# A streamed fp32 matmul with scale and add on one core: 28 transfers in place of 39, and the last pairs of tiles off TensorE

## The chip, the core and the metric

The kernel runs on one core of a Trainium2 chip. A core has TensorE (PE in the profile, with its weight loads shown apart as PEld), VectorE (DVE), ScalarE (ACT), GpSimd (POOL) and SyncE (SP); here SP does nothing but issue the transfers between the chip's main memory and the on-chip memory, and 16 DMA engines carry them. The metric is the device time of the launch in microseconds, lower is better. Each kernel is timed in several runs and the median is taken; one more execution is recorded by the hardware profiler.

## The reference

```python
batch, m, k, n = 16, 512, 1024, 768
x          = randn(batch, m, k)   # float32
weight     = randn(k, n)          # float32
scale      = 0.1
add_value  = randn(batch, m, n)   # float32

return (scale * np.matmul(x, weight) + add_value).astype(np.float32)
```

With the batch flattened, `x` is 8192 x 1024 and the output 8192 x 768. A tile is 128 rows, so there are T = 64 tiles. In float32, a tile of `x` has 0.524 MB, a tile of `add_value` or of the output 0.393 MB, and `weight` has 3.15 MB. All data crosses the memory once: 33.55 MB of `x`, 25.17 MB of `add_value`, 3.15 MB of `weight`, 25.17 MB of output, 87.03 MB in all.

## The kernel before

**Layout.** `rows` views the rows in groups of 8 tiles (G = 8): inside a group a partition holds 8 neighbouring rows of memory, one for each tile. So a transfer of n tiles of one group reads, for each of the 128 partitions, one run of n rows: 4,096 bytes times n for `x`, 3,072 bytes times n for `add_value` and the output.

**Buffers.** `xs` has 16 slots for tiles of `x` in fp32 (tile t lies in slot t % 16). `ao` has 32 slots of 768 columns, which hold `add_value`, are overwritten in place by the result, and are stored from there (tile t in slot t % 32). At the start the last 8 slots of `ao` take the fp32 weight, and the three before them (21 to 23, `EARLY_AT`) the scaled products of the first three tiles. `w_bf` is the weight in bf16.

**Work on a tile.** The product needs `x` with k on the partitions, in bf16. There are two ways to it.

- *Through TensorE*: POOL (for the first three tiles DVE with ACT or POOL) casts the tile to bf16 (`cast_to`, L130; `xb_pool` has 3 buffers), TensorE transposes it in 4 pieces, taking two bf16 values as one fp32 (`transpose`, L156), and DVE or ACT copies the result from PSUM to `xt` (L164). ACT does the copy for tiles 0 to 3 and, before, for the tiles after the last moved pair.
- *Off TensorE* (a moved pair, `move_pair` and `turn_moved`): ACT or POOL casts two tiles in 16 instructions of 32 partitions x 512 elements, four in each of four steps, which also moves 32-row blocks between partitions (L118), and DVE turns 32 x 32 blocks in one instruction (L126). `MOVED_ACT` and `MOVED_POOL` list the first tiles of these pairs; each of the two engines has two buffers (`va_pool`, `vp_pool`).

A tile's product is 16 matmuls (8 steps of k, 512 and 256 columns each), into one of 3 PSUM buffers (`mm_pool`). `finish` (L185) is one DVE instruction: product times scale plus `ao`, written to `ao`.

**Order.** The order is written out by hand. `STREAM` lists all transfers: `x` and `w` load, `a` loads `add_value`, `o` stores the output (`l` and `r`: its left and right columns). SP issues them in this order, and a transfer whose slots are not free yet holds up those behind it. The loop at L248 walks through the list and, ahead of each entry, emits as many steps of the computation as the entry needs: a load of `x` over slots in use needs all their casts and moves, a store needs `finish` of its tiles. A load of `add_value` over slots in use waits for the store from them to land.

`head` does the first three tiles (EARLY = 3) while the weight comes in, one k step at a time, with `add_value` added afterwards (`added`, L245). From tile 3 on, `step` does one tile t: half of its matmuls, the transposes of tile t + 1 if that isn't in a moved pair, the casts up to tile t + 4, a quarter of the move of the pairs that start at t + 8, t + 7, t + 6 and t + 5, the other half of the matmuls, `finish`, and last, if a moved pair starts at t + 4, its turn on DVE. So on DVE the turn of pair t + 4 stands between `finish` of t and `finish` of t + 1. The last tile's matmuls and `finish` are split by columns.

Of the kernel before, what the change touches and what calls it, by code (L numbers as in the profile page):

```python
# [9 lines left out]


STREAM = [
    ("x", 0, 3), ("w", 0, 2), ("w", 2, 2), ("w", 4, 2), ("x", 3, 1), ("w", 6, 2),
    ("a", 0, 3), ("x", 4, 4), ("a", 3, 1), ("a", 4, 4), ("x", 8, 4), ("x", 12, 4),
    ("x", 16, 4), ("a", 8, 8), ("x", 20, 4), ("x", 24, 8), ("o", 0, 8), ("a", 16, 8),
    ("x", 32, 8), ("a", 24, 8), ("a", 32, 8), ("x", 40, 8), ("o", 8, 8), ("x", 48, 8),
    ("a", 40, 8), ("o", 16, 8), ("x", 56, 8), ("a", 48, 8), ("o", 24, 8), ("o", 32, 8),
    ("a", 56, 8), ("o", 40, 8), ("o", 48, 8), ("o", 56, 4), ("o", 60, 1), ("o", 61, 1),
    ("o", 62, 1), ("l", 63, 1), ("r", 63, 1),
]  # L20

X_SLOTS = 16
# [3 lines left out]
EARLY = 3  # L26

MOVED_ACT = [14, 18, 22, 26, 30, 34, 38, 42, 46, 50, 54, 58]  # L30
MOVED_POOL = [16, 20, 24, 28, 32, 36, 40, 44, 48, 52, 56]


@with_exitstack
def kernel(
# [8 lines left out]
    nc = tc.nc  # L44
    P = 128
# [19 lines left out]
    def rows(view, s, n):  # L65
        assert s // G == (s + n - 1) // G
        return view[:, s // G, s % G:s % G + n, :]


    w_v = weight.rearrange("(c p r) n -> p c r n", p=P, r=2)  # L70

    const = ctx.enter_context(tc.tile_pool(name="const", bufs=1))
    xb_pool = ctx.enter_context(tc.tile_pool(name="xb_pool", bufs=XB_BUFS))
# [12 lines left out]
    ao = const.tile([P, A_SLOTS, N], fp32, name="ao")  # L86
    w_bf = const.tile([P, KJ, N], bf16, name="w_bf")

    xb_tiles, xt_tiles, mm_tiles, done = {}, {}, {}, {"cast": 0, "step": 0, "x": 0}
    in_pair = {t0 + i: t0 for t0 in MOVED_ACT + MOVED_POOL for i in range(2)}  # L90
    moved, cast_pairs = {}, set()

    def load_w(j, n):

        s = A_SLOTS - KJ + j
        if n == 1:
            nc.sync.dma_start(ao[:, s, :], w_v[:, j // 2, j % 2, :])
        else:
            nc.sync.dma_start(ao[:, s:s + 2, :], w_v[:, j // 2, :, :])  # L99
        for i in range(n):  # L100
            nc.vector.tensor_copy(w_bf[:, j + i, :], ao[:, s + i, :])  # L101

    def move_pair(t0, a):


        act = t0 in MOVED_ACT
        if a == 0:
# [22 lines left out]
    def cast_to(t):  # L130
        while done["cast"] <= t:
            i = done["cast"]
            if i in in_pair:
                assert in_pair[i] in cast_pairs
                done["cast"] += 1
                continue
            if len(xb_tiles) == XB_BUFS:
                break
            xb = xb_pool.tile([P, K], bf16, tag="xb")
            src = xs[:, i % X_SLOTS, :]  # L140
            if i < EARLY:
                nc.vector.tensor_copy(xb[:, 0:K // 2], src[:, 0:K // 2])  # L142
                other = nc.gpsimd.tensor_copy if i else nc.scalar.copy
                other(xb[:, K // 2:K], src[:, K // 2:K])  # L144
            else:
                nc.gpsimd.tensor_copy(xb, src)  # L146
            xb_tiles[i] = xb
            done["cast"] += 1

    def transpose(t, pieces=1):  # L150
        cast_to(t)

        pairs = xb_tiles.pop(t).bitcast(fp32)
        tp = tp_pool.tile([P, KC, P], fp32, tag="tp")
        for c in range(KC):
            nc.tensor.transpose(tp[:, c, :], pairs[:, c * P:(c + 1) * P], identity)  # L156
        if t % 2 == 0:
            xt = xt_pool.tile([P, 2, KC, P], fp32, tag="xt")
            for i in range(2):
                xt_tiles[t + i] = xt[:, i, :, :]  # L160
        q = KC // pieces
        evacuate = nc.scalar.copy if t <= EARLY or t > LAST_PAIR else nc.vector.tensor_copy
        for c in range(0, KC, q):
            evacuate(  # L164
                xt_tiles[t][:, c:c + q, :].bitcast(bf16), tp[:, c:c + q, :].bitcast(bf16))
# [25 lines left out]
    def head(op, s, n):  # L191


        for i in range(s, s + n):
            if op == "x" and i < EARLY:
                transpose(i, 2)
                have_x.append(i)
                for j in have_w:
                    product(i, j, BOTH)
            elif op == "w":  # L200
                if i == KJ - 1:
                    transpose(EARLY)
                have_w.append(i)
                for t in have_x:
                    product(t, i, BOTH)
        if len(have_w) == KJ and len(have_x) == EARLY and not done["step"]:
            for t in range(EARLY):

                if t == 1:
                    nc.scalar.mul(  # L210
                        ao[:, EARLY_AT + t, :], mm_tiles[t, BOTH[0]][:, 0:N], float(scale))
                else:
                    nc.vector.tensor_scalar(  # L213
                        ao[:, EARLY_AT + t, :], mm_tiles[t, BOTH[0]][:, 0:N], float(scale), None,
                        op0=mybir.AluOpType.mult)
            done["step"] = EARLY

    LAST_PAIR = max(in_pair)
    EARLY_AT = A_SLOTS - KJ - EARLY

    def step():
        t = done["step"]
        if t < T - 1:
            for j in range(KJ):
                if j == KJ // 2:
                    if t + 1 not in in_pair:
                        transpose(t + 1)
                    cast_to(min(t + AHEAD, done["x"] - 1))
                    for a in range(4):
                        if in_pair.get(t + 8 - a) == t + 8 - a:  # L230
                            move_pair(t + 8 - a, a)
                product(t, j, BOTH)
            finish(t, BOTH[0], 0, N)
            if in_pair.get(t + 4) == t + 4:
                turn_moved(t + 4)
        else:
            for cols in BOTH:
                for j in range(KJ):
                    product(t, j, [cols])
                finish(t, cols, *cols)  # L240
        done["step"] += 1

    def added(t):
        assert done["step"] >= EARLY
        nc.vector.tensor_add(  # L245
            ao[:, t, :], ao[:, EARLY_AT + t, :], ao[:, t, :])

    for op, s, n in STREAM:  # L248
        last = s + n - 1
        if op == "w":  # L250
            load_w(s, n)
            head(op, s, n)
        elif op == "x":
            if last >= X_SLOTS:
                while done["cast"] <= last - X_SLOTS:
                    step()
            k = s % X_SLOTS
            nc.sync.dma_start(xs[:, k:k + n, :], rows(x_v, s, n))  # L258
            done["x"] = s + n
            if last < EARLY:  # L260
                head(op, s, n)
        elif op == "a":
            k = s % A_SLOTS
            nc.sync.dma_start(ao[:, k:k + n, :], rows(add_v, s, n))  # L264
            for t in range(s, min(s + n, EARLY)):
                added(t)
        else:
            while done["step"] <= last:
                step()
            k = s % A_SLOTS  # L270
            n0, n1 = {"o": (0, N), "l": (0, CUT), "r": (CUT, N)}[op]
            nc.sync.dma_start(rows(out_v, s, n)[:, :, n0:n1], ao[:, k:k + n, n0:n1])  # L272
# [35 lines left out]
```

## Time and profile before

| | |
|---|---|
| median of 3 runs | 210.14 us (209.95 to 210.92) |
| the profiled execution | 210.28 us |
| its span, first to last instruction | 208.5 us |
| TensorE busy, granted clock (mean) | 181.6 us, 0.96 |
| DVE, ACT, POOL busy | 101.3, 129.0, 124.3 us |
| DMA: bytes, mean rate over the span | 87.21 MB, 418 GB/s |
| transfers in `STREAM` | 39 |

The span is what the profile covers; the device time of the same execution is 1.8 us longer. Busy time is the time in which an engine executes instructions; for the 16 DMA engines it is the mean over them. The profile's page has, beside these, a picture of the span in 40 slices of 5.2 us, the share of each DMA queue, the chain of waits that ended last, and the groups of instructions by line; the trace also holds each transfer's issue, each packet's size and duration, and the moment at which each of the 16 engines finished its part of a transfer.

### The profile page before, as it was taken

The numbers are of one execution on the slowest core, as the hardware profiler recorded it, in microseconds if no ns is written. First come the engines' busy times: TensorE is split into PE (matmuls) and PEld (weight loads), VectorE is DVE, ScalarE is ACT, GpSimd is POOL, SyncE is SP. The second block draws the span as 40 slices with busy tenths as digits, with TensorE's granted clock in tenths as the row PEclk, the third lists the DMA queues.
The fourth block names the chain that finished last, engine by engine and source line by source line (L and its number), as shares of the span: only waits on it lengthen the run. The fifth ranks groups of instructions, "written<-read, shape, count | busy, mean of one in ns | idle before, by whom it ended". The sixth has DMA issues, their size and how long they took to land.

```text
span 208.5 us, 2886 instructions
## 1 busy us (share of the span) xinstructions
PE 181.6 (87%) x1096; PEld 110.7 (53%) x1096; DVE 101.3 (49%) x111; ACT 129.0 (62%) x206; POOL 124.3 (60%) x199
## 2 busy tenths in 40 slices
PE   0599399980899997999999999999999999989960
PEld 0455256650466664566666666666666666656630
DVE  0536535511466514855655555555553685233330
ACT  2423000499959798599999999999999900003210
POOL 1310524379898980999998899999999960001000
PEclk9999889996589999999999999999999999999997
DMA  6999999999999999999999999999999999999995
GB/s 236 415 428 440 413 429 434 421 450 406 454 418 448 407 429 462 404 443 420 442 434 413 461 418 424 420 429 437 421 434 424 432 439 424 429 418 439 429 394 214
DMA packets 5629, 87.21 MB, mean 418 GB/s; under 512 B 624, under 2 KB 752, under 8 KB 2032
## 3 DMA queue, kind: packets, MB, share of 16 engines
q1 hardware_dynamic: 5616, 87.03, 98.2%
q8 instruction: 8, 0.13, 0.3%
q14 instruction: 5, 0.04, 0.0%
HBM read 61.87 MB, written 25.17 MB: 417 GB/s over the span
## 4 chain that ended last, share of the span: by engine, by line
DMA 75%; ACT 9%; PE 7%; DVE 3%; SPq 1%; issue 1%; DVEq 0%
DMA out_dram<-ao 35%; DMA ao<-in_add_value_dram 22%; DMA xs<-in_x_dram 13%; ACT va L118 9%; PE mm L177 6%; DMA ao<-in_weight_dram 5%; DVE ao L185 2%; DVE xt L126 1%; PE tp L156 1%; SPq L258 1%; SPq L99 0%; SPq L264 0%; SPq L272 0%; DVEq L185 0%
## 5 line engine op out<-in xcount | busy, mean ns | idle before, releaser
L177 PE MATMUL mm<-w_bf,xt 128*128 128x256 bf16 (+1 forms) x1024 | 173.8, 331 | 8.8 <-DVE xt L164 6.6
L177 PEld LDWEIGHTS <-xt 128*128 128x128 bf16 x1024 | 101.3, 99 | 76.9 <-DVE xt L164 7.0
L118 ACT CAST va<-xs 32x512 bf16<-32x512 f32 x192 | 118.2, 616 | 28.8 <-DMA xs<-in_x_dram 19.1
L118 POOL CAST va<-xs 32x512 bf16<-32x512 f32 x176 | 106.8, 607 | 15.9 <-DVE xt L126 6.2
L185 DVE SCALAR_TENSOR_TENSOR ao<-mm,ao 128x768 f32<-128x768 f32 (+2 forms) x62 | 58.1, 942 | 78.1 <-PE mm L177 49.1
L146 POOL CAST xb<-xs 128x1024 bf16<-128x1024 f32 x15 | 15.2, 1040 | 43.4 <-PE tp L156 22.5
L164 ACT COPY xt<-tp 128x512 bf16<-128x512 bf16 (+1 forms) x11 | 8.2, 785 | 35.3 <-PE tp L156 35.3
L126 DVE STREAM_TRANSPOSE xt<-va 128x1024 f32<-128x1024 f32 x23 | 28.4, 1234 | 0.0
L156 PE MATMUL tp<-identity,xb 128*128 128x128 f32 x72 | 12.9, 314 | 11.2 <-DVE xb L142 7.4
L156 PEld LDWEIGHTS tp<-identity,xb 128*128 128x128 f32 x72 | 9.8, 161 | 13.7 <-issue 7.6
L164 DVE COPY xt<-tp 128x1024 bf16<-128x1024 bf16 x10 | 6.9, 686 | 10.1 <-PE tp L156 10.1
L101 DVE CAST w_bf<-ao 128x768 bf16<-128x768 f32 x8 | 4.1, 556 | 3.8 <-DMA ao<-in_weight_dram 3.8
L142 DVE CAST xb<-xs 128x512 bf16<-128x512 f32 x3 | 1.9, 696 | 6.8 <-DMA xs<-in_x_dram 6.8
L144 POOL CAST xb<-xs 128x512 bf16<-128x512 f32 x2 | 1.6, 834 | 5.5 <-DMA xs<-in_x_dram 5.5
L144 ACT CAST xb<-xs 128x512 bf16<-128x512 f32 x1 | 0.6, 618 | 4.8 <-DMA xs<-in_x_dram 4.8
L213 DVE TENSOR_SCALAR ao<-mm 128x768 f32<-128x768 f32 x2 | 1.8, 952 | 1.9 <-PE mm L177 1.9
L245 DVE TENSOR_TENSOR ao<-ao 128x768 f32<-128x768 f32 x3 | 2.7, 951 | 0.0
L144 ACT ACT_TABLE_LOAD x1 | 1.3, 1283 | 0.7 <-PEq L289 0.7
L210 ACT ACTIVATE ao<-mm 128x768 f32<-128x768 f32 x1 | 0.8, 817 | 0.0
masks.py:197 POOL MEMSET identity<- 128x128 f32 x1 | 0.2, 204 | 0.3 <-POOLq L289 0.3
masks.py:199 POOL TENSOR_SCALAR_AFFINE_SELECT identity<-identity 128x128 f32<-128x128 f32 x1 | 0.3, 292 | 0.1
L289 POOL MEMSET const-float32-0.0<- 128x1 f32 x1 | 0.1, 98 | 0.2 <-issue 0.2
(3 smaller groups left out, 0.3 us busy)
## 6 DMA issues: line engine op xcount, KB each, us to landing
ao<-in_add_value_dram SPq DMA_DIRECT2D x7, 3072.0 KB, 26.1
out_dram<-ao SPq DMA_DIRECT2D x7, 3072.0 KB, 23.9
xs<-in_x_dram SPq DMA_DIRECT2D x5, 4096.0 KB, 18.8
xs<-in_x_dram SPq DMA_DIRECT2D x5, 2048.0 KB, 26.6
ao<-in_weight_dram SPq DMA_DIRECT2D x4, 768.0 KB, 9.6
xs<-in_x_dram SPq DMA_DIRECT2D x1, 1536.0 KB, 6.1
ao<-in_add_value_dram SPq DMA_DIRECT2D x1, 1536.0 KB, 19.3
out_dram<-ao SPq DMA_DIRECT2D x1, 1536.0 KB, 12.9
```

Source lines behind the costliest of these rows:

```text
L101: nc.vector.tensor_copy(w_bf[:, j + i, :], ao[:, s + i, :])
L118: move(moved[t0][32 * b:32 * b + 32, :, a, :], src[32 * a:32 * a + 32, :, b, :])
L126: nc.vector.transpose(xt.rearrange("p i c m -> p (i c m)"), moved.pop(t0).bitcast(fp32).rearrange("p c a k -> p (c a k)"))
L142: nc.vector.tensor_copy(xb[:, 0:K // 2], src[:, 0:K // 2])
L144: other(xb[:, K // 2:K], src[:, K // 2:K])
L146: nc.gpsimd.tensor_copy(xb, src)
L156: nc.tensor.transpose(tp[:, c, :], pairs[:, c * P:(c + 1) * P], identity)
L164: evacuate(xt_tiles[t][:, c:c + q, :].bitcast(bf16), tp[:, c:c + q, :].bitcast(bf16))
L177: nc.tensor.matmul(mm_tiles[t, cols[0]][:, n0:n1], lhs(t, j), w_bf[:, j, n0:n1], start=(j == 0), stop=(j == KJ - 1))
L185: nc.vector.scalar_tensor_tensor(a, mm_tiles[t, part][:, n0:n1], float(scale), a, op0=mybir.AluOpType.mult, op1=mybir.AluOpType.add)
L245: nc.vector.tensor_add(ao[:, t, :], ao[:, EARLY_AT + t, :], ao[:, t, :])
L258: nc.sync.dma_start(xs[:, k:k + n, :], rows(x_v, s, n))
```

## The change

`STREAM` is replaced: 28 transfers. The first load brings tiles 0 to 3, the weight comes in two halves of 4 k steps, then `add_value` 0 to 7, `x` 4 to 7, and from there groups of eight in another order of loads and stores; the last eight tiles are stored as five and three. `load_w` can take any even number of k steps in one transfer. `head` is called for a load of `x` that starts below tile 3 (it still does tiles 0 to 2 alone). Pairs 62 and 60 are appended to `MOVED_ACT` and `MOVED_POOL`, so no tile from 14 on is transposed by TensorE, and the special case of ACT's copy for the last tiles goes, with `LAST_PAIR`.

```diff
--- before.py
+++ after.py
@@ -10,13 +10,11 @@
 
 
 STREAM = [
-    ("x", 0, 3), ("w", 0, 2), ("w", 2, 2), ("w", 4, 2), ("x", 3, 1), ("w", 6, 2),
-    ("a", 0, 3), ("x", 4, 4), ("a", 3, 1), ("a", 4, 4), ("x", 8, 4), ("x", 12, 4),
-    ("x", 16, 4), ("a", 8, 8), ("x", 20, 4), ("x", 24, 8), ("o", 0, 8), ("a", 16, 8),
-    ("x", 32, 8), ("a", 24, 8), ("a", 32, 8), ("x", 40, 8), ("o", 8, 8), ("x", 48, 8),
-    ("a", 40, 8), ("o", 16, 8), ("x", 56, 8), ("a", 48, 8), ("o", 24, 8), ("o", 32, 8),
-    ("a", 56, 8), ("o", 40, 8), ("o", 48, 8), ("o", 56, 4), ("o", 60, 1), ("o", 61, 1),
-    ("o", 62, 1), ("l", 63, 1), ("r", 63, 1),
+    ("x", 0, 4), ("w", 0, 4), ("w", 4, 4), ("a", 0, 8), ("x", 4, 4), ("x", 8, 8),
+    ("a", 8, 8), ("x", 16, 8), ("a", 16, 8), ("a", 24, 8), ("x", 24, 8), ("o", 0, 8),
+    ("x", 32, 8), ("o", 8, 8), ("x", 40, 8), ("a", 32, 8), ("o", 16, 8), ("a", 40, 8),
+    ("x", 48, 8), ("a", 48, 8), ("x", 56, 8), ("o", 24, 8), ("o", 32, 8), ("a", 56, 8),
+    ("o", 40, 8), ("o", 48, 8), ("o", 56, 5), ("o", 61, 3),
 ]
 
 X_SLOTS = 16
@@ -27,8 +25,8 @@
 
 
 
-MOVED_ACT = [14, 18, 22, 26, 30, 34, 38, 42, 46, 50, 54, 58]
-MOVED_POOL = [16, 20, 24, 28, 32, 36, 40, 44, 48, 52, 56]
+MOVED_ACT = [14, 18, 22, 26, 30, 34, 38, 42, 46, 50, 54, 58, 62]
+MOVED_POOL = [16, 20, 24, 28, 32, 36, 40, 44, 48, 52, 56, 60]
 
 
 @with_exitstack
@@ -67,7 +65,7 @@
         return view[:, s // G, s % G:s % G + n, :]
 
 
-    w_v = weight.rearrange("(c p r) n -> p c r n", p=P, r=2)
+    w_v = weight.rearrange("(c p r) n -> p c (r n)", p=P, r=2)
 
     const = ctx.enter_context(tc.tile_pool(name="const", bufs=1))
     xb_pool = ctx.enter_context(tc.tile_pool(name="xb_pool", bufs=XB_BUFS))
@@ -93,10 +91,10 @@
     def load_w(j, n):
 
         s = A_SLOTS - KJ + j
-        if n == 1:
-            nc.sync.dma_start(ao[:, s, :], w_v[:, j // 2, j % 2, :])
-        else:
-            nc.sync.dma_start(ao[:, s:s + 2, :], w_v[:, j // 2, :, :])
+        assert j % 2 == n % 2 == 0
+        nc.sync.dma_start(
+            ao[:, s:s + n, :].rearrange("p (c r) n -> p c (r n)", r=2),
+            w_v[:, j // 2:(j + n) // 2, :])
         for i in range(n):
             nc.vector.tensor_copy(w_bf[:, j + i, :], ao[:, s + i, :])
 
@@ -159,7 +157,7 @@
             for i in range(2):
                 xt_tiles[t + i] = xt[:, i, :, :]
         q = KC // pieces
-        evacuate = nc.scalar.copy if t <= EARLY or t > LAST_PAIR else nc.vector.tensor_copy
+        evacuate = nc.scalar.copy if t <= EARLY else nc.vector.tensor_copy
         for c in range(0, KC, q):
             evacuate(
                 xt_tiles[t][:, c:c + q, :].bitcast(bf16), tp[:, c:c + q, :].bitcast(bf16))
@@ -215,7 +213,6 @@
                         op0=mybir.AluOpType.mult)
             done["step"] = EARLY
 
-    LAST_PAIR = max(in_pair)
     EARLY_AT = A_SLOTS - KJ - EARLY
 
     def step():
@@ -257,7 +254,7 @@
             k = s % X_SLOTS
             nc.sync.dma_start(xs[:, k:k + n, :], rows(x_v, s, n))
             done["x"] = s + n
-            if last < EARLY:
+            if s < EARLY:
                 head(op, s, n)
         elif op == "a":
             k = s % A_SLOTS
```

## The prediction

> **What bounds the kernel now.** I looked first at the page's head, its engine shares, the DMA row of the 40 slices and the queue's share.
>
> ```profile
> span 208.5 us, 2886 instructions
> ...
> PE 181.6 (87%) x1096; PEld 110.7 (53%) x1096; DVE 101.3 (49%) x111; ACT 129.0 (62%) x206; POOL 124.3 (60%) x199
> ...
> DMA  6999999999999999999999999999999999999995
> ...
> q1 hardware_dynamic: 5616, 87.03, 98.2%
> ```
>
> The DMA engines are busy from the first slice to the last. The first packet starts at 1.8 us, the last store has landed at 207.59. The next view is the stages (columns: window, length, busy time and count of PE, PEld, DVE, ACT, POOL, clock, DMA share, GB/s).
>
> ```profile
> 100.00:150.00 50.00, 50.00 (x309) 30.11 (x308) 28.88 (x30) 48.59 (x80) 46.05 (x76) 1.00 1.00 430
> 150.00:186.00 36.00, 36.00 (x222) 21.63 (x221) 18.10 (x19) 16.39 (x27) 18.82 (x30) 1.00 1.00 429
> 186.00:203.00 17.00, 14.96 (x97) 9.23 (x95) 7.30 (x9) 4.05 (x4) 1.04 (x1) 1.00 0.99 422
> 203.00:208.50 5.50, 0.00 (x0) 0.00 (x0) 0.00 (x0) 0.00 (x0) 0.00 (x0) 0.74 0.56 221
> ```
>
> The DMA share is 1.00 at 430 GB/s; in the last 5.5 us no engine computes and the queue drains. Then the end of the timeline:
>
> ```profile
> 185.67 2.69 DVE L185 SCALAR_TENSOR_TENSOR ao<-mm,ao 128x768 f32<-128x768 f32 x3 [6.42 <-DMA ao<-in_add_value_dram]
> ...
> 197.72 1.01 ACT L164 COPY xt<-tp 128x1024 bf16<-128x1024 bf16 x1 [2.02 <-PE tp L156]
> ...
> 201.62 0.42 DVE L185 SCALAR_TENSOR_TENSOR ao<-mm,ao 128x256 f32<-128x256 f32 x1 [0.18 <-PE mm L177]
> ```
>
> The last result is ready at 202.04, and the last store still waits behind queued ones: it lands 5.5 us after its issue. So the compute chain at the end of the chain of waits isn't what sets the end. What it and the SP waits are good for is to tell when a transfer can be issued:
>
> ```profile
> SPq L258 <- ACT va L118: 90.1, 5, 22.0
> SPq L264 <- DMA out_dram<-ao: 40.1, 4, 23.2
> ```
>
> SP waits for moves that free slots of `xs`, and for stores to land; it is ahead of the DMA engines all the time, else their row would have gaps.
>
> The 16 engines don't finish together. For the last store the trace has the first at 205.17 and the last at 207.59: a lag of 2.42 us. It is 0.38 until 28 us, and jumps to 1.7 beside a 16,384-byte instruction fetch (1.06 us) at 30.4. Eight such fetches come in the run, and by the end about 12 engines lag 0.7 us or more. The slowest engine sets the end.
>
> **What the Trainium skill says.** "DMA: Bandwidth & Descriptors", section "Where 436 GB/s comes from", puts the ceiling at 435.2 GB/s; the trace agrees: 24,576-byte packets take 912 ns (431 GB/s over 16 engines). Section "Why small descriptors are slow (HBM only)" tells of a fixed cost for each packet; medians of the trace show it: 1,024 bytes 46 ns, 2,048 84, 3,072 122, 6,144 234.5, 9,216 352, 12,288 461, 16,384 614, 24,576 912, 32,768 1,213. Section "Measured (HBM→SBUF, 128 partitions, SWDGE, issued from GpSimd)" advises transfers of 1 MiB or more. Here that isn't where time is lost: the single-tile stores of 384 KB land 0.95 us apart (418 GB/s), so what one transfer costs by itself is hidden behind those queued. Section "Why a DMA increments its semaphore by 16 and not by 1" says that the engines of a transfer finish independently; the lag above agrees.
>
> **The change part by part.**
>
> *Packets.* A transfer has one run of bytes for each of the 128 partitions (a weight half has two), and each run is a packet, so each of the 16 engines carries 8 packets of it. Before, one engine's sum: 8 x 46 + 8 x 84 + 32 x 122 + 8 x 159 (4,096) + 32 x 234.5 + 8 x 352 + 24 x 461 + 40 x 614 + 112 x 912 + 40 x 1,213 ns = 202.8 us, and 39 semaphore writes of 9 ns, 0.35. After: 16 x 614 + 56 x 1,213 (`x`) + 120 x 912 (seven stores and eight `add_value` loads of eight) + 8 x 577 (15,360 bytes, between its neighbours: bounds 562 and 590) + 8 x 352 + 32 x 234.5 (weight: the runs stay 6,144 bytes) = 202.1, and 28 x 9 ns, 0.25. Saved: 0.77 us. The start is left at no gain: first issue at 0.74, first packet at 1.8, and first packets that take some 1.1 us[...].
>
> *Is the queue still never empty?* I add up the bytes in the new order and read when before had landed the same number (32.5 MB at 80.8, 42.99 MB at 103.0 on the first engine and 105.1 on the last, 77.59 MB at 185.57), less 0.3 to 0.7 us for the packets saved by then; between such points the slope is 0.4265 MB/us. Each transfer must be issued about 1.06 us (0.74 to 1.8 above) before the one ahead of it is drained.
>
> Head: tiles 0 to 3 land at 8.0, the weight at 15.6 as before (same 5.24 MB), `add_value` at 23, tiles 4 to 7 at 28 (before: 23.3). Tile 3 can't end before 32.6, 4.5 us later; but tile 8 no longer stalls on its `add_value` (before: 8.6 us of DVE wait), so tile 10 comes out at 54, near the time before. POOL's four casts (3.99) free `xs` for x(16,8) at 32.0; the queue holds x(8,8) and a(8,8) until 46.
>
> x(24,8): POOL's cast of 13 stands behind four moves of pair 16, whose data land at 56: 56 + 2.6 + 1.04 = 59.6; queue until 69. x(32,8): pair 16 and cast 13 end at 67.4, pair 20 at 77.8; queue until 86.
>
> x(40,8) is the tight one. It needs pairs 24 and 28 (POOL) and 26 and 30 (ACT) moved. x(24,8) lands at 32.5 MB, 80.5. POOL's rate:
>
> ```profile
> 83.05 31.20 POOL L118 CAST va<-xs 32x512 bf16<-32x512 f32 x48 [5.38 <-DVE xt L126]
> 114.92 52.04 POOL L118 CAST va<-xs 32x512 bf16<-32x512 f32 x80 [0.67 <-DMA xs<-in_x_dram]
> ```
>
> 0.65 us an instruction, 10.4 a pair: 80.5 + 20.8 = 101.3 (ACT at 0.629: 100.6), first packet 102.4. The engines have drained what lies ahead (42.99 MB) at 102.6 (fastest) to 104.7 (slowest): no gap. All later loads have 7 us or more: x(48,8) at 122 against 136, x(56,8) at 143 against 153, a(56,8) once o(24,8) lands at 171 against 178.
>
> *Pairs 60 and 62.* Off PE: four tiles' transposes, 0.44 each in the chain, 1.76 in all; off ACT four copies of 1.01; off POOL four casts of 1.04. On: 16 moves each on ACT (10.06) and POOL (10.4), two turns of 1.24 on DVE. a(56,8) lands at 184.9 (before 185.57, the same 77.59 MB), so `finish` of 56 ends at 185.9. Behind it in DVE's order waits the turn of pair 60, for POOL: x(48,8) lands at 146, four pairs, 187.6, turned at 188.8. `finish` of 57, 58, the turn of 62 follow to 191.7. PE, which waits behind these for buffers, has 56 to 58 in its three, ends 59 by 189.6 in that of 56, and goes on at 2.6 a tile: 63 ends at 200.1, `finish` at 200.6, against 202.04. `finish` of 60 is done by 194.
>
> None of this costs time as long as the queue covers it; uncovered, pair 60's chain would be on the path one for one.
>
> *Tail.* o(56,5) is issued at 194, o(61,3) at 200.7, first packet 201.7. The slowest engine drains what is ahead at 206.8 - 8 x 352 ns = 204.0, the fastest at 201.6: cover is 2.3 us on the engine that counts. The last piece, 9,216 bytes a run and not 1,024, costs nothing beyond its bytes, since all engines are still busy.
>
> *Sum.* Span 208.5 - 0.77 = 207.7; 210.28 - 0.77 = 209.5 for that execution. Its time was 0.14 over the median, so **209.4** against 210.14: -0.35%, inside the 0.5% (1.05 us, 209.09 to 211.19) that a measurement of this kernel tells from no change.
>
> **Rivals.**
>
> *A: x(40,8) comes too late and the queue runs dry (slower).* Place: SP's wait for the moves of pairs 24 to 30, about 101 us. Up to 2.3 us of delay is taken by the slowest engine's lag; beyond that each us costs one. It passes 211.19 from 2.3 + 1.8 = 4.1 us, which is 0.78 an instruction on POOL in place of 0.65, or pair 24 starting at 84.6. For it: POOL and ACT move without a pause, and before this transfer had 7.5 us. Against: durations of moves are 603 to 612 and 613 to 621 ns throughout. With 6 us: 213.
>
> *B: POOL's chain sets the tail.* Pairs 48 to 60 take 41.6 us in a row. If 60 is turned 4.5 us later, everything after it is: 200.6 becomes 205.1, o(61,3) starts 2.2 us late: 211.6. Against: only the landing of x(48,8) would move it.
>
> *C: the lag shrinks (faster).* Lag is luck of which engine gets the fetches. If no engine gets more than one, the lag falls from 2.42 to about 1.5: 208.5. For it: PE's program shrinks by 16 transposes. Against: 32 of 2,192 instructions hardly change eight fetches.
>
> *D: nothing is saved.* If the shared ceiling and not the packet limits the rate, or the lag grows by what the packets give: 210.1.
>
> **How the numbers follow.** Forecast 0.43 (its own range 209.0 to 209.9), A 0.13, B 0.07, C 0.22, D 0.15. Faster: C and a little of the forecast, 0.25; slower: A and B, 0.20; the rest, 0.55. The range takes in C and D and the lower part of A and B: 208.5 to 211.2. The unknown costs (15,360-byte packet 0.2 us, fetches -0.9 to +0.8) lie inside.
>
> **What would show it.** Right: DMA nines throughout, q1 some 0.7 us (of engine time) below before's, x(40,8) issued near 101, the last `finish` near 200.6, the last store landing near 206.8. Wrong: a slice with a 7 or 8 near 102 or 200; SP's wait on L258 ending after 105; a POOL move pace above 0.7; landings ahead of these times in the middle of the run, which would mean that the rate itself rose.

## The result, and the profile after

The changed kernel takes 211.93 us (median of 4 runs, 211.72 to 212.09), the kernel before 210.12 in the same comparison: a ratio of 1.0078, 95% interval 1.005 to 1.0105. It is slower by 0.8%. The forecast was 209.4, and 211.93 lies outside the range up to 211.2.

The profiled execution took 211.72 us, with a span of 209.9. The head of its page, the DMA row and the queue's share:

```profile
span 209.9 us, 2860 instructions
...
PE 180.3 (86%) x1080; PEld 108.9 (52%) x1080; DVE 101.9 (49%) x113; ACT 134.9 (64%) x218; POOL 130.1 (62%) x211
...
DMA  6999999999999999999999999999999999999994
...
q1 hardware_dynamic: 4288, 87.03, 97.7%
```

The DMA row is all nines again: in slices of 5.2 us and with nine standing for 90% or more, it can't show what happened. Shorter windows can (columns as in the prediction's stages; the last two are DMA share and GB/s). Changed kernel:

```profile
90.00:101.00 11.00, 7.96 (x51) 4.70 (x49) 5.89 (x6) 10.78 (x18) 10.25 (x18) 1.00 1.00 428
101.00:106.00 5.00, 5.00 (x33) 3.00 (x31) 4.22 (x5) 4.90 (x8) 4.64 (x9) 1.00 0.93 352
106.00:118.00 12.00, 12.00 (x76) 7.23 (x74) 6.61 (x7) 11.76 (x21) 11.20 (x19) 1.00 1.02 438
118.00:123.00 5.00, 4.30 (x27) 2.46 (x26) 0.00 (x0) 4.91 (x8) 4.64 (x9) 1.00 0.94 338
```

Kernel before, the same two short windows:

```profile
101.00:106.00 5.00, 5.00 (x33) 3.05 (x32) 2.87 (x4) 4.89 (x9) 4.64 (x9) 1.00 1.02 436
118.00:123.00 5.00, 5.00 (x33) 3.00 (x31) 3.07 (x3) 4.91 (x9) 4.65 (x9) 1.00 1.00 428
```

There are two holes: 352 and 338 GB/s over 5 us each, where the kernel before has 436 and 428. At 430 GB/s that is roughly (430 - 352) x 5 / 430 = 0.9 us and (430 - 338) x 5 / 430 = 1.1 us; roughly, because this view counts a packet whole in the window in which it starts. With each packet divided over the windows that it spans, the packet records give 356 and 363 GB/s, 0.9 and 0.8 us, and a busy share of 0.94 in the first hole and 0.99 in the second: only in the first do engines stand still. Elsewhere the rates are alike.

What stands at the first hole is seen in SP's timeline of the changed kernel (issue time, length, line, transfer):

```profile
77.75 0.33 SPq L255 DMA_DIRECT2D xs<-in_x_dram  x1
...
101.77 0.33 SPq L255 DMA_DIRECT2D xs<-in_x_dram  x1
102.15 0.42 SPq L261 DMA_DIRECT2D ao<-in_add_value_dram  x1
102.66 0.38 SPq L269 DMA_DIRECT2D out_dram<-ao  x1
105.12 0.33 SPq L261 DMA_DIRECT2D ao<-in_add_value_dram  x1
```

At 101.77 SP issues x(40,8) (the load of the 8 tiles from 40 on; the others are named alike), then a(32,8), o(16,8) and a(40,8). The first packet of x(40,8) starts at 102.73. The engines ran out of o(8,8) from 102.31 on, so they stood still for 0.33 us in the mean, and on most of them the first packet of x(40,8) then took 1.5 to 2.3 us where 1.21 is usual. The second hole is the end of a(32,8): its last packet of eight took 1.0 to 1.7 us in place of 0.91, and on some engines the one before it up to 2.2, just ahead of the turn to o(16,8).

The chain of waits now looks quite different, and misleads. Before and after, by engine:

```profile
DMA 75%; ACT 9%; PE 7%; DVE 3%; SPq 1%; issue 1%; DVEq 0%
```

```profile
DMA 34%; PE 29%; POOL 26%; issue 6%; SPq 1%; DVE 1%; POOLq 0%; DVEq 0%
```

It follows the issue of the last store back through the last result to TensorE and POOL. But the slowest DMA engine lost nothing there (-0.07 us), so that chain set when the last store was issued and not when it landed.

The trace has for every transfer the moment at which each of the 16 engines reported its part as landed. That is some 0.3 to 0.6 us after the end of the engine's last packet (o(8,8), fastest engine: 102.31 and 102.80). The mean over the engines of the step from one transfer's landing to the next, less the packets' own times, is a transfer's *loss*. It is +0.81 us at x(40,8) and +0.82 at a(32,8); all other transfers after the first are between -0.17 and +0.21 (kernel before: -0.08 to +0.19). For the slowest engine the balance at the same number of bytes is:

| bytes landed | before | after | difference |
|---|---|---|---|
| 22.02 MB | 56.12 | 55.75 | -0.37 |
| 42.99 MB (ahead of x(40,8)) | 105.09 | 105.05 | -0.04 |
| 47.19 MB (after x(40,8)) | 114.80 | 115.03 | +0.23 |
| 50.33 MB (after a(32,8)) | 122.10 | 123.66 | +1.56 |
| 77.59 MB (a(56,8)) | 185.57 | 187.00 | +1.43 |
| 87.03 MB (end) | 207.59 | 208.85 | +1.26 |

### The profile page after: what moved, and what is told of

Same layout as the page of the kernel before. It is cut to its first block, busy times and chain, and to the rows that moved or that the text cites. A ratio compares the mean times of both kernels' runs of the same rounds, so it can differ in the third digit from the quotient of the medians.

```text
span 209.9 us, 2860 instructions
## 1 busy us (share of the span) xinstructions
PE 180.3 (86%) x1080; PEld 108.9 (52%) x1080; DVE 101.9 (49%) x113; ACT 134.9 (64%) x218; POOL 130.1 (62%) x211
## 3 DMA queue, kind: packets, MB, share of 16 engines
q1 hardware_dynamic: 4288, 87.03, 97.7%
## 4 chain that ended last, share of the span: by engine, by line
DMA 34%; PE 29%; POOL 26%; issue 6%; SPq 1%; DVE 1%; POOLq 0%; DVEq 0%
DMA xs<-in_x_dram 34%; PE mm L175 27%; POOL va L116 24%; PE tp L154 2%; POOL xb L144 1%; DVE ao L183 1%; SPq L95 0%; SPq L261 0%; SPq L255 0%; POOLq L144 0%; POOLq L116 0%; DVE xt L124 0%; DVEq L183 0%
## 5 line engine op out<-in xcount | busy, mean ns | idle before, releaser
L116 ACT CAST va<-xs 32x512 bf16<-32x512 f32 x208 | 128.1, 616 | 36.2 <-DMA xs<-in_x_dram 33.7
L116 POOL CAST va<-xs 32x512 bf16<-32x512 f32 x192 | 116.6, 607 | 23.5 <-DMA xs<-in_x_dram 15.2
L183 DVE SCALAR_TENSOR_TENSOR ao<-mm,ao 128x768 f32<-128x768 f32 (+2 forms) x62 | 56.8, 928 | 26.1 <-PE mm L175 16.6
L124 DVE STREAM_TRANSPOSE xt<-va 128x1024 f32<-128x1024 f32 x25 | 30.9, 1235 | 47.3 <-POOL va L116 47.3
L144 POOL CAST xb<-xs 128x1024 bf16<-128x1024 f32 x11 | 11.2, 1042 | 28.5 <-DMA xs<-in_x_dram 23.9
L154 PE MATMUL tp<-identity,xb 128*128 128x128 f32 x56 | 10.2, 318 | 13.7 <-DVE xb L140 8.8
L154 PEld LDWEIGHTS tp<-identity,xb 128*128 128x128 f32 x56 | 7.6, 163 | 15.9 <-issue 8.7
L162 ACT COPY xt<-tp 128x512 bf16<-128x512 bf16 (+1 forms) x7 | 4.1, 655 | 10.2 <-PE tp L154 10.2
```

Of the source, the lines that this page charges most:

```text
L116: move(moved[t0][32 * b:32 * b + 32, :, a, :], src[32 * a:32 * a + 32, :, b, :])
L124: nc.vector.transpose(xt.rearrange("p i c m -> p (i c m)"), moved.pop(t0).bitcast(fp32).rearrange("p c a k -> p (c a k)"))
L162: evacuate(xt_tiles[t][:, c:c + q, :].bitcast(bf16), tp[:, c:c + q, :].bitcast(bf16))
L183: nc.vector.scalar_tensor_tensor(a, mm_tiles[t, part][:, n0:n1], float(scale), a, op0=mybir.AluOpType.mult, op1=mybir.AluOpType.add)
```

## The experiments

Theory T1: both losses come from the late issue of x(40,8). T2: the second has a cause of its own, in what is transferred there. T3: the second is luck. Losses are those of the profiled execution, "turn" is the load straight ahead of the next store; lead is the time from the issue of the late load to the moment at which the fastest engine's part of the transfer ahead had landed; that engine had run out of packets 0.3 to 0.6 us sooner.

| run | lead, us | loss at the late load | loss at the turn | median, us | ratio to before (95%) |
|---|---|---|---|---|---|
| changed kernel | 1.0 | x(40,8) 0.81 | a(32,8) 0.82 | 211.93 | 1.0078 (1.005 to 1.0105) |
| e1, once more | 0.7 | x(40,8) 0.83 | a(32,8) 1.12 | 212.36 | 1.0112 (1.0095 to 1.0129) |
| e2, a(32,8) first | 8.0 | x(40,8) 0.00 | none | 210.35 | 1.0010 (1.0003 to 1.0017) |
| e3, before with the new tail | | none | none | 210.12 | 0.9991 (0.9979 to 1.0002) |
| e4, x(40,8) later | -2.0 | x(40,8) 3.24 | a(32,8) 1.21 | 214.51 | 1.0212 (1.0192 to 1.0232) |
| e5, x(24,8) ahead of a(24,8) | 1.6 | x(24,8) 0.34 | a(24,8) 1.28 | 211.07 | 1.0050 (1.0034 to 1.0066) |
| e6, o(16,8) ahead of a(32,8) | 0.9 | x(40,8) 1.87, both in one | | 217.76 | 1.0367 (1.032 to 1.0415) |
| e7, before with x(40,8) early in the order | -0.3 | x(40,8) 2.00 | a(32,8) 1.08 | 214.05 | 1.0204 (1.0169 to 1.0238) |
| e8, 8 moves less | 6.7 | x(40,8) -0.10 | a(32,8) 0.02 | 210.20 | 1.0005 (0.9995 to 1.0015) |
| e9, 2 moves less | 2.9 | x(40,8) -0.11 | a(32,8) 0.10 | 211.01 | 1.0041 (1.0027 to 1.0055) |
| e10, 4 moves less | 3.8 | x(40,8) -0.11 | a(32,8) 0.00 | 209.99 | 0.9996 (0.9988 to 1.0005) |
| e11, DVE does 8 moves | 3.0 | x(40,8) 0.02 | a(32,8) 0.36 | 210.45 | 1.0010 (0.9998 to 1.0023) |

### e1: the changed kernel once more

> The changed kernel once more, for a second trace. Its first trace loses, in the mean over the 16 DMA engines and against its packets' own times, 0.81 us at x(40,8) and 0.82 us at the transfer behind it, a(32,8), about 119 to 121 us. Theory T1 (both come from x(40,8) being issued too late): both losses are there again, together 1.4 to 1.8 us, median 211.7 to 212.1. Theory T2 (the second loss is of its own, tied to what is transferred there): both again as well. Theory T3 (the second loss is luck): x(40,8) loses 0.8 again, a(32,8) loses under 0.2, and the median of other executions would be near 211.2.

212.36 us, a little over the forecast. Both losses are there again, 0.83 and 1.12: not luck, T3 is out. T1 and T2 stay.

### e2: a(32,8) ahead of x(40,8)

```diff
-    ("x", 32, 8), ("o", 8, 8), ("x", 40, 8), ("a", 32, 8), ("o", 16, 8), ("a", 40, 8),
+    ("x", 32, 8), ("o", 8, 8), ("a", 32, 8), ("x", 40, 8), ("o", 16, 8), ("a", 40, 8),
```

> The changed kernel with a(32,8) put ahead of x(40,8), so that the queue has 7.3 us more work when x(40,8) is issued (still about 101.8). T1: no loss at either, last landing near 207.2, median 210.1 to 210.5, and 209.5 if the engines' lag shrinks as well. T2: x(40,8) loses nothing but 0.8 us are lost again about 120 us or at a(32,8): median 210.9 to 211.4. If neither loss is what makes the kernel slow: 211.7 to 212.1.

x(40,8) is issued at 102.02, no sooner than in the changed kernel, but the queue now has 7.3 us more to do. The two windows of this run:

```profile
101.00:106.00 5.00, 5.00 (x33) 3.04 (x31) 3.97 (x4) 4.89 (x9) 4.64 (x9) 1.00 1.00 428
118.00:123.00 5.00, 5.00 (x33) 2.95 (x31) 1.01 (x2) 3.93 (x8) 4.64 (x9) 1.00 1.01 428
```

Both holes are gone, and the median falls to 210.35, as T1 said. What this run can't exclude is that the neighbours matter, since a(32,8) no longer stands ahead of o(16,8).

### e3: the new tail on the kernel before

```diff
-    ("a", 56, 8), ("o", 40, 8), ("o", 48, 8), ("o", 56, 4), ("o", 60, 1), ("o", 61, 1),
-    ("o", 62, 1), ("l", 63, 1), ("r", 63, 1),
+    ("a", 56, 8), ("o", 40, 8), ("o", 48, 8), ("o", 56, 5), ("o", 61, 3),
...
-MOVED_ACT = [14, 18, 22, 26, 30, 34, 38, 42, 46, 50, 54, 58]
-MOVED_POOL = [16, 20, 24, 28, 32, 36, 40, 44, 48, 52, 56]
+MOVED_ACT = [14, 18, 22, 26, 30, 34, 38, 42, 46, 50, 54, 58, 62]
+MOVED_POOL = [16, 20, 24, 28, 32, 36, 40, 44, 48, 52, 56, 60]
```

> The kernel before with the tail of the changed one alone: pairs 60 and 62 moved off TensorE, the last eight tiles stored as five and three. My forecast's part for it: the packets of the last stores save about 0.16 us, the last result 1.5 us earlier or so saves nothing: 209.9 to 210.2. If the tail is what makes the changed kernel slow (fast engines 0.26 us idle ahead of the last store there): 210.6 to 211.9.

210.12 against 210.16: no change that can be measured. Moving pairs 60 and 62, and storing five and three tiles, is neither the loss nor a gain.

### e4: x(40,8) still later

```diff
+        if a == 3 and t0 == 28:
+            for b in range(4):
+                nc.gpsimd.tensor_copy(
+                    moved[t0][32 * b:32 * b + 32, :, a, :], src[32 * a:32 * a + 32, :, b, :])
```

> The changed kernel with the last four moves of pair 28 done twice on POOL, so that x(40,8) is issued 2.6 us later (104.4). T1: the slowest engine has no cover left, so the last landing is 2.0 to 2.6 us later: median 213.9 to 214.5. T2 and T3: the same for the first loss, since all of them hold that the queue runs dry there. If the 2.3 us of lag still cover the delay, as the prediction had it: under 0.5 us more, 211.9 to 212.4.

x(40,8) is issued at 104.75, the median is 214.51: 2.6 us over the changed kernel's 211.93 for 2.98 us of delay (against e1, taken together with it, 2.2 us for 2.7). Two windows of this run, at the issue and 16 us later:

```profile
104.00:108.00 4.00, 3.04 (x19) 1.75 (x18) 3.25 (x4) 3.93 (x7) 3.70 (x7) 1.00 0.75 260
120.00:126.00 6.00, 5.31 (x34) 3.09 (x32) 0.15 (x1) 5.87 (x11) 5.59 (x10) 1.00 0.98 339
```

The second hole has moved with the first: the slow packets of a(32,8), from 118.6 in the changed kernel, here begin at 121.4. Its loss, 1.21, doesn't grow with the first one (3.24).

### e5: x(24,8) ahead of a(24,8)

```diff
-    ("a", 8, 8), ("x", 16, 8), ("a", 16, 8), ("a", 24, 8), ("x", 24, 8), ("o", 0, 8),
+    ("a", 8, 8), ("x", 16, 8), ("a", 16, 8), ("x", 24, 8), ("a", 24, 8), ("o", 0, 8),
```

> The changed kernel with x(24,8) put ahead of a(24,8): the same bytes lie ahead of x(40,8), but tiles 24 to 31 land 7.3 us sooner (73.7), are moved 7 us sooner, and x(40,8) is issued near 94.8, 8 us before the engines have drained what is ahead. a(32,8) still lies between x(40,8) and o(16,8). T1 (the loss at a(32,8) follows from the gap at x(40,8)): both losses under 0.25 us, last landing 207.0 to 207.5, median 210.0 to 210.4. T2 (a load of add_value straight ahead of that store is slow of itself): x(40,8) loses nothing, a(32,8) still 0.8 to 1.2, median 211.0 to 211.5.

This missed in a way that helps. x(40,8) was issued at 99.0 (not 94.8: POOL was still moving pair 20 until about 78, which I had left out), and it and a(32,8) lose nothing (-0.11 and 0.10), though a(32,8) does stand between it and o(16,8): T2 is out. But x(24,8) is now issued at 59.77, with a lead of 1.6 us, and loses 0.34; and a(24,8) behind it, ahead of o(0,8), loses 1.28:

```profile
75.00:80.00 5.00, 4.95 (x32) 3.01 (x31) 1.91 (x2) 4.89 (x9) 4.68 (x8) 1.00 1.01 326
```

A small loss at a late load brings the second with it, at another place, with other data. And no engine stood still at x(24,8): on each, its first packet starts within 0.02 us of the end of what lay ahead. Still 14 of the 16 first packets took 1.47 to 2.12 us. So neither the slow first packets nor the second loss needs a standstill; an issue that is too late is enough. The median, 211.07, is that of T2's forecast, for another reason.

### e6: o(16,8) ahead of a(32,8)

```diff
-    ("x", 32, 8), ("o", 8, 8), ("x", 40, 8), ("a", 32, 8), ("o", 16, 8), ("a", 40, 8),
+    ("x", 32, 8), ("o", 8, 8), ("x", 40, 8), ("o", 16, 8), ("a", 32, 8), ("a", 40, 8),
```

> The changed kernel with o(16,8) ahead of a(32,8), behind the late x(40,8). x(40,8) loses 0.8 to 1.1 us as before. T1: a second loss comes with it again, now at x(40,8)'s own end or at o(16,8), 0.5 to 1.2 us: median 211.7 to 212.3. T2: no load of add_value stands ahead of the store, so no second loss: median 210.9 to 211.4.

Windows of this run: the issue of x(40,8), its own end, and the tail.

```profile
101.00:106.00 5.00, 4.95 (x32) 2.95 (x32) 4.30 (x5) 4.91 (x9) 4.64 (x9) 1.00 0.94 349
108.00:115.00 7.00, 6.95 (x44) 4.25 (x44) 3.81 (x4) 6.86 (x12) 6.51 (x12) 1.00 0.99 363
196.00:206.00 10.00, 9.95 (x63) 6.01 (x62) 4.59 (x6) 0.00 (x0) 0.00 (x0) 1.00 0.49 209
```

The second hole is now inside x(40,8), at its end, which is here straight ahead of the store: it sits at the turn from loads to stores, whichever load that is. The time, 217.76, was in nobody's numbers: a(32,8) lands at 131.7 and not at 123.7, all of the computation behind it slips, o(56,5) is issued only at 204.2 and loses 4.9 us, o(61,3) another 2.6. With 8 us of slip the compute chain is the bound, but not POOL's chain of rival B. TensorE waits 9 us for `finish` of tile 32 and is busy nearly without a pause from there to the end:

```profile
132.79 7.58 PE L175 MATMUL mm<-w_bf,xt 128*128 128x512 bf16 x29 [8.97 <-DVE ao L183]
```

### e7: the same fault put into the kernel before

```diff
-    ("x", 32, 8), ("a", 24, 8), ("a", 32, 8), ("x", 40, 8), ("o", 8, 8), ("x", 48, 8),
+    ("x", 32, 8), ("a", 24, 8), ("x", 40, 8), ("a", 32, 8), ("o", 8, 8), ("x", 48, 8),
```

> The kernel before with a(32,8) put behind x(40,8), nothing else: x(40,8) is still issued near 96.0 and the engines have drained what is ahead of it at 95.4 (fastest) to 97.5 (slowest), as in the changed kernel. T1: x(40,8) loses 0.8 to 1.3 us and a(32,8), now straight ahead of o(8,8), 0.8 to 1.2 more: median 211.6 to 212.3. If only the gap counts and the second loss belongs to the changed order: 210.9 to 211.3. If a gap of this size is covered by the engines' lag: 210.1 to 210.5.

x(40,8) is issued at 95.91 as in the kernel before, now 0.3 us after the fastest engine has finished. Windows:

```profile
94.00:100.00 6.00, 5.95 (x38) 3.60 (x37) 3.61 (x4) 5.88 (x10) 5.57 (x11) 1.00 0.78 285
100.00:111.00 11.00, 10.95 (x69) 6.59 (x69) 6.50 (x7) 10.78 (x19) 10.29 (x17) 1.00 0.99 428
111.00:117.00 6.00, 5.95 (x38) 3.67 (x38) 3.66 (x4) 5.88 (x10) 5.55 (x11) 1.00 1.02 360
```

Both holes, 2.00 and 1.08, and 214.05 us. The pattern needs nothing of the change but a load issued too late. My size was too low: 2.0 and not 0.8 to 1.3 at x(40,8).

### e8, e9, e10: the changed kernel's own order, x(40,8) issued sooner

```diff
+        if t0 in (28, 30) and a == 3:
+            nc.vector.memset(moved[t0][0:128, :, a, :], 0.0)
         for b in range(4):
+            if t0 in (28, 30) and a == 3:
+                continue
             move = nc.scalar.copy if act else nc.gpsimd.tensor_copy
```

This is e10 (4 of 16 moves left out in the pairs that x(40,8) waits for); e8 has `a >= 2` (8 left out), e9 `a == 3 and b >= 2` on partitions 64 to 127 (2 left out).

> The changed kernel with its own order of transfers; of pairs 28 and 30 only half the moves are made (8 of 16 each), and DVE fills the rest of the two buffers with zeros, so four tiles of the product are left incomplete. x(40,8) is issued near 96.5 in place of 101.8, nothing else in the queue is altered. If the late issue of x(40,8) is the cause of both losses: x(40,8) and a(32,8) lose under 0.25 us each in the mean over the engines, median 210.0 to 210.5. If the order itself (a load of add_value between x(40,8) and o(16,8)) causes the second one: a(32,8) still loses 0.8 to 1.2, median 211.0 to 211.5.

> As the run with half the moves, with 14 of 16 moves made in pairs 28 and 30: x(40,8) is issued near 100.5, 1.8 us before the fastest engine has drained what is ahead (102.3; the slowest 104.6). If a lead of 1.0 us, from issue to first packet, is enough, as my prediction had it: no loss, median 210.0 to 210.5. If more lead is needed because the first packets of a load after a standstill are slow: x(40,8) loses 0.2 to 0.6 and a(32,8) 0.8 to 1.2 as well, median 211.2 to 211.8.

> As the last two, with 12 of 16 moves made in pairs 28 and 30: x(40,8) is issued near 99.2, 3.1 us before the fastest engine has drained what is ahead. A lead of 3 us should be enough in either view: no loss at x(40,8), and none at a(32,8) if the second follows from the first: median 210.0 to 210.5. If the second loss has a cause of its own: 211.0 to 211.5.

x(40,8) is issued at 96.20, 100.11 and 99.15. e8 and e10 have no holes and run at 210.20 and 209.99. The windows of e10:

```profile
101.00:106.00 5.00, 4.95 (x32) 3.02 (x31) 2.87 (x4) 4.91 (x9) 4.65 (x9) 1.00 1.02 439
118.00:123.00 5.00, 4.95 (x32) 2.95 (x31) 0.95 (x2) 4.89 (x9) 4.64 (x9) 1.00 0.99 421
```

With the order of transfers untouched, 2.6 us on one issue are worth 1.9 us of the median (211.93 to 209.99), and both losses go together. These three runs alter the work of POOL, ACT and DVE and not the order; e2 alters the order and not the work; both ways bring the time back. In e10 no first packet of x(40,8) is slow (1.23 us at most). e9 stands on the edge, between its two forecasts: its profiled execution (210.47) has no hole and two slow first packets, but its 20 runs spread from 209.99 to 212.38, median 211.01, where the kernel before spreads from 209.91 to 210.67. About 3 us of lead is still not always enough.

### e11: a complete kernel with the sooner issue

```diff
             move = nc.scalar.copy if act else nc.gpsimd.tensor_copy
+            if t0 in (28, 30) and a == 0:
+                move = nc.vector.tensor_copy
```

> The changed kernel, complete, with the first quarter of the moves of pairs 28 and 30 (four each) given to DVE, which waits idle at that time: POOL and ACT have 12 moves each there, as in the run with four moves less, and x(40,8) is issued near 99.2. If the lead of x(40,8) is the cause: no loss at x(40,8) and a(32,8), last landing near 207.0, median 209.8 to 210.2, a ratio to before of 0.998 to 1.001. If DVE's moves delay a turn that POOL or TensorE waits for: 210.5 or more. If the full saving of the packets (0.77 us) comes out: 209.3 to 209.6.

x(40,8) is issued at 99.92, 0.8 us later than in e10, and again on the edge: five of its 16 first packets take 1.4 to 2.0 us, 0.36 us are lost at a(32,8), the runs go from 209.85 to 211.13. The median, 210.45, lies above the forecast. DVE's moves are not seen to delay the end: at the last store the slowest engine loses nothing (-0.07). This kernel takes back most of the loss, and is not faster than the kernel before.

## Why the prediction was wrong

*The bound*: right. In every run the time follows when the DMA engines finish; TensorE, DVE, ACT and POOL don't set it, except in e6, where TensorE does.

*When each load of `x` is issued*: right to about half a us. x(16,8) 32.04 (forecast 32.0), x(24,8) 59.48 (59.6), x(32,8) 77.75 (77.8), x(40,8) 101.77 (101.3), x(48,8) 122.6 (122), x(56,8) 143.5 (143). POOL's pace carried it; the changed kernel's timeline has

```profile
80.95 62.49 POOL L116 CAST va<-xs 32x512 bf16<-32x512 f32 x96 [3.24 <-DMA xs<-in_x_dram]
```

which is 0.651 us an instruction against 0.65.

*The step that failed* is x(40,8): "first packet 102.4. The engines have drained what lies ahead (42.99 MB) at 102.6 (fastest) to 104.7 (slowest): no gap." The times in it were good to 0.5 us, the place was the one I had named as tight, and rival A named the place where the queue runs dry. Three terms were wrong or missing. First, the moments of draining were read from landings, and the engines run out of packets about half a us before that: in the changed kernel the fastest at 102.31 (landing at 102.80). With the first packet at 102.73 that made 0.33 us of standstill in the mean, where the sum had "no gap". Second, the first packets of a load issued so late are slow (1.5 to 2.3 us for 1.21), in e5 even where no engine stands still. I took the 1.06 us from issue to first packet as a sufficient lead, the one value that the trace of before shows, at a start from nothing; I had slow first packets in the start's sum, where both kernels have them, and not here. The runs show losses at leads of 1.6 us and less, none at 3.8 and more, and a mixed picture at 3. The packets' own time on an engine, which was to fall by some 0.7 us, rose from 204.7 to 205.1 (203.9 in e10, without the holes): most of what was lost went into slow packets. Third, and on the slowest engine the largest, the second loss at the turn to the next store, 0.8 to 1.3 us, which no case had. Rival A's sentence "Up to 2.3 us of delay is taken by the slowest engine's lag" did hold for the first hole: there the fastest engine lost 1.03 us and the slowest 0.27. It did not hold for the second, where all engines lose and the slowest lost 1.33. So A's outcome came at a delay that A called free.

*The packets*: 0.77 us were to be saved (the terms of the sum come to 0.79). Without the holes (e8, e10, e2) the mean engine finishes the last store at 205.98, 206.06 and 206.20 us against 206.41 before: 0.2 to 0.4 us. The packets themselves took what I had summed (15,360 bytes: 573 ns, forecast 577). But the sum lays their durations end to end, while in the traces a packet starts some 4 ns before the one ahead of it on its engine ends. With 83 records fewer on each engine (351 and 268, semaphore writes included) that is 0.3 us that was never there to save, and 0.4 to 0.5 us are left, near what e8 and e10 show. In the medians not even this can be told from no change (e10: 0.9996, e8: 1.0005, e2: 1.0010). That is rival D's number; neither of its reasons is seen, since the packets were not slower and the lag didn't grow (at the last store 1.9 us in e8 and 1.7 in e10, 2.4 before).

*Pairs 60 and 62, and the tail*: the chain was as described, about 2 us later behind the holes. The turn of pair 60 and the last result in the changed kernel:

```profile
189.72 1.25 DVE L124 STREAM_TRANSPOSE xt<-va 128x1024 f32<-128x1024 f32 x1 [1.67 <-POOL va L116]
...
202.46 0.42 DVE L183 SCALAR_TENSOR_TENSOR ao<-mm,ao 128x256 f32<-128x256 f32 x1 [0.18 <-PE mm L175]
```

x(48,8) landed at 147.94 and not at 146, so the turn ended at 190.97 (forecast 188.8); a(56,8) landed at 187.00 and not at 184.9, and the last result came at 202.88 (200.6). The fastest engine then lost 0.26 us ahead of the last store and the slowest nothing (-0.07): that cover was real. In e2 the fastest lost 1.01 there, and the slowest again nothing. e3 confirms that the tail changes nothing by itself.

*Rival C*: the lag hardly shrank: 2.28 us at o(56,5) against 2.42 there before, and 1.95 at the last store because the fastest engine had waited for it. It wasn't C's 1.5, and the holes cost more than it gave.

## What to carry to other kernels

In a kernel bound by its transfers, list for every transfer when it can be issued and when the engines run out of what is ahead of it, which is before its landing. In this kernel a lead of 1.0 us cost 0.8%, about 3 us was sometimes too little, and 3.8 us cost nothing; what another kernel needs is not shown here. Where a load waits for buffers, put a transfer that waits for nothing ahead of it: a(32,8) ahead of x(40,8), one swap in a list, took the time from 211.93 back to 210.35. And look at the DMA rate in windows of 5 us around each late issue and the next turn to a store, since a row of nines hides two holes of a us: in the second no engine even stands still, its packets are slow.

## What the runs showed of the hardware that I had not expected

- After a load issued too late, the next turn from loads to stores cost 0.8 to 1.3 us in the mean over the engines, 8 to 16 us after the load's first packet (changed kernel, e1, e4, e5, e7; in e6 it is some 1.1 of the 1.87). It sits on the last packets of the load ahead of the store, whichever load that is, and hardly depends on how much the late load lost (first loss 0.34 to 3.24, second 0.82 to 1.28) or on whether an engine stood still (e5: none did). Other turns cost up to 0.3 us. It goes with the slow first packets of the late load: of 16, none in e10, two in e9 and five in e11, with 0.00, 0.10 and 0.36 us lost at a(32,8). What makes the engines slow there isn't known from these runs.
- One trace does not settle a lead near the edge: the kernel of e9, with a lead of 2.9 us in its profiled execution, ran between 209.99 and 212.38 us.
- A gap that only the early engines see was free ahead of the last store: 1.01 us on the fastest engine (e2), -0.07 on the slowest.
